# Memory gates kept in SBUF until the output stage, with other buffers, accumulators and preparation order there

## The chip, the cores and the metric

The kernel runs on one core of a Trainium2 chip. The metric is the device time of one execution in microseconds (us). Before the change three runs gave 604.79, 606.60 and 608.34 us. One further execution was profiled; its own time is 606.42 us, and the span of its trace is 604.6 us, so 1.8 us lie outside the span.

## The reference, cut to what matters

```
def merge(x, fox_o, gf, pool_o, gp, mem_o, gm, w_out):
    cat = concatenate([silu(gf) * fox_o,      # 512 columns, forgetting attention
                       silu(gp) * pool_o,     # 256 columns, pooling mixer
                       silu(gm) * mem_o])     # 256 columns, memory attention
    return x + cat @ w_out                    # then y = rmsnorm(., g_final)
```

There are 1024 prompt rows and 64 sample rows of width 1024. One input projection gives queries, keys, values, forget gates, the pooling path and the three gates gf, gp, gm. Eight forgetting-attention heads (prompt rows causal over 1024 keys, sample rows over 512 cached keys and their own), four memory heads and the pooling mixer give 1024 columns in all; these are gated, multiplied by w_out, added to x and normalised. All of it is float32.

## The kernel before, in words

Each float32 matrix product is made of products of rounded halves: every operand is split into a high part (names ending in `hi`, or `wh`, `xh`, `chi`) and a low part (`lo`, `wl`, `xl`, `clo`), and three matmuls per block of 128 (high times high, high times low, low times high) are added up in PSUM.

Nothing is scheduled by hand. Every instruction goes to a `Planner` that records its reads and writes, then `flush` (line 189) places all instructions in one order by a cost model: at each step it takes the instruction that can start first on its engine, and among those that can start together the one with the lower `rank`, then the longer remaining path. `add` (line 94) gives rank -1 to matmuls into the PSUM pools `ps`, `pt` and `po`, and to work of other engines that touches pools `pp` or `wp`; all else has rank 0. The order is then fixed: each engine, and the DMA queue of SyncE (SP), takes its instructions one after the other and waits where one of them must wait. Tiles come from rings: a tile with 2 buffers can be written again when the readers of the tile two allocations earlier are done.

After the input projections and the attention heads, two things end the program. `proj2` (line 612) projects the two 128-column tiles of the memory gate gm, for three chunks of rows in the order `LAST` = (2, 1, 0): rows 768 to 1087, 256 to 767, 0 to 255. `gate_tile` (line 676) makes the gate: a multiply (`gr`, DVE), a Tanh (`gt`, ACT), a combine (DVE), and a store to DRAM (`gated`).

The output stage follows. `load_wout` (line 1204) loads w_out in three column blocks (blocks 1, 0 and 2 in that order; 256, 512 and 256 columns) in 8 pieces, and splits each into `wh` (ACT cast) and `wl` (a subtraction on POOL in two parts, or on DVE). These take the SBUF of the x halves, so block 1 can be written when chunk 2 of the projection is done, block 0 after chunk 1, block 2 after chunk 0. Raw pieces go by turns to a tile `wr` (one buffer) and to a `ptile` `Q` (three buffers).

`out_prep(t)` (line 1151) prepares a row tile t of 128 rows (t = 8 is the 64 sample rows) in two halves of four 128-column blocks: DMA of the attention results (`catd`), of the reciprocal row sums (`rsd`) and of the gates (`gated`), a multiply by the row sums (DVE), a multiply by the gates (POOL), a cast to `chi` (ACT) and a subtraction to `clo` (DVE). `chi` and `clo` take the `whi` and `wlo` rings of pool `wp`, two buffers each, which the projection weights use before. `out_tile(t)` (line 1231) does the matmuls into PSUM, for the columns in three steps (columns 768 to 1023, 0 to 511, 512 to 767), adds x (tile `xt`), sums squares (ACT), takes the root, scales and stores. Both accumulators of a tile come from pool `pp` (two banks). The tiles are taken in the order 8, 0, 1, ..., 7, and the last one ends with three separate steps.

Of the kernel before, what the change touches and what calls it, by code (L numbers as in the profile page):

```python
# [42 lines left out]
class Planner:  # L43
# [5 lines left out]
    def __init__(self, nc, tc):  # L49
        self.nc, self.tc = nc, tc  # L50
        self.ops = []
        self.acc = {}
        self.slots = {}
        self.alloc = {}
        self.users = {}
        self.home = {}
        self.free = {e: 0.0 for e in self.ENG}
        self.lock = {"vector": 0.0, "gpsimd": 0.0}
        self.mode = self.table = None
        self.dma = [0.0] * 16  # L60
        for e in self.ENG:
            setattr(self, e, _Eng(self, e))
# [31 lines left out]
    def add(self, eng, fn, args, kw):  # L94
# [12 lines left out]
        urgent = into & {"ps", "pt", "po"} if eng == "tensor" else "pp" in homes or "wp" in into  # L107
        op.rank = -1 if urgent else 0
        preds = set()
# [162 lines left out]
def tile_hymba_step(  # L272
# [45 lines left out]
    def half(par):  # L318
# [4 lines left out]
    md = [dram.tile([4 * HD, 2 * MEM], F32, name=f"md{j}") for j in range(2)]  # L323
    gated = [
        [dram.tile([r, n], F32, name=f"gated{r}_{t0}") for t0, n in CH] for r in (768, 256)
    ]
    catd = [dram.tile([D, 256 if c < 4 else NSA], F32, name=f"catd{c}") for c in range(5)]
# [347 lines left out]

    def gate_tile(r0):
        def f(acc, ci, t0, n):
            t = row("gr")
            nc.vector.tensor_tensor(t[:, :n], acc[:, :n], rb[:, t0 : t0 + n], op=ALU.mult)
            th = row("gt")  # L680
            nc.scalar.activation(th[:, :n], t[:, :n], AF.Tanh, scale=0.5)
            nc.vector.scalar_tensor_tensor(
                t[:, :n], th[:, :n], 1.0, t[:, :n], op0=ALU.add, op1=ALU.mult
            )
            g, r = divmod(r0, 768)
            nc.sync.dma_start(gated[g][ci][r : r + P, :n], t[:, :n])

        return f
# [462 lines left out]
    def out_prep(t):  # L1151
# [4 lines left out]
        hk = lambda x, w: x[:, : w * m].rearrange("p (k t) -> p k t", k=w)  # L1156
        ch = kv(wp.tile([P, WC], F32R, tag="whi", name=nm("chi")))
        if t < 8:
            cl = kv(wp.tile([P, WC], F32R, tag="wlo", name=nm("clo")))
        else:  # L1160
            cl = ch[:, :, m:]
        w = 512 // m
        rt = ptile()[:, : 6 * m].rearrange("p (k t) -> p k t", k=6)
        for par in (0, 1):
# [6 lines left out]
        for a in range(0, KT, w):  # L1171
            ct, gt = hk(ptile(512), w), hk(ptile(512), w)
            nc.sync.dma_start(
                ct, catd[t // 2][a * P : (a + w) * P, oc : oc + m].rearrange("(k p) t -> p k t", p=P)
            )
            for g, e0, e1 in ((0, 0, 6), (1, 6, 8)):
                b0, b1 = max(a, e0), min(a + w, e1)
                if b0 < b1:
                    nc.sync.dma_start(
                        gt[:, b0 - a : b1 - a, :],  # L1180
                        gated[g][ci][(b0 - e0) * P : (b1 - e0) * P, o : o + m].rearrange(
                            "(k p) t -> p k t", p=P
                        ),
                    )
            ks = slice(a, a + w)
            for b0, b1, o0 in ((0, 4, 0), (6, 8, 2)):
                b0, b1 = max(a, b0), min(a + w, b1)
                if b0 < b1:
                    c_ = ct[:, b0 - a : b1 - a, :]
                    nc.vector.tensor_tensor(c_, c_, rt[:, b0 - o0 : b1 - o0, :], op=ALU.mult)  # L1190
            nc.gpsimd.tensor_tensor(ct, ct, gt, op=ALU.mult)
            nc.scalar.activation(ch[:, ks, :m], ct, AF.Copy, scale=0.5)
            nc.vector.scalar_tensor_tensor(
                cl[:, ks, :m], ct, 0.5, ch[:, ks, :m], op0=ALU.mult, op1=ALU.subtract
            )
# [8 lines left out]
    def load_wout():  # L1204
        gfb.append(ap_.tile([P, UW], F32, tag="u", name="gfb", bufs=1)[:, :D])
        nc.sync.dma_start(gfb[0], gfin.unsqueeze(0).to_broadcast([P, D]))
        for ci in LAST:
# [6 lines left out]
            for i, k0 in enumerate(range(0, KT, kk)):  # L1214
                raw = ptile() if i % 2 else wp.tile([P, D], F32, tag="wr", name=nm("wr"), bufs=1)
                raw = raw.rearrange("p (k c) -> p k c", k=kk)
# [14 lines left out]
    def out_tile(t):  # L1231
# [17 lines left out]
        for pi, pc, o, w, full in steps:  # L1249
            if pi not in accs:  # L1250
                accs[pi] = ppt() if pi < 2 else pst()
            acc = accs[pi]
# [30 lines left out]
        for nh in (0, 1):  # L1283
# [9 lines left out]
            else:  # L1293
                nc.scalar.activation(xg[:, cols], xg[:, cols], AF.Copy, scale=r)
                nc.scalar.dma_start(y_o[c, cols], xg[:, cols])

    def project(name):
        kind, j = name[:-1], int(name[-1])
# [5 lines left out]
        elif kind == "k":  # L1304
            proj(TK + j, k_tile(j))
        elif kind == "gf":
            proj(TGF + j, gate_tile(j * P))
        elif kind == "qm":
            proj(TQM + j, q_tile(4 + j))
        elif kind == "u":  # L1310
            proj(TU + j, u_tile(j))
        elif kind == "gp":
            proj(TGP + j, gate_tile(512 + j * P))
        else:
            proj2(TGM, gate_tile(768), TGM + 1, gate_tile(768 + P))

# [32 lines left out]
    for _ in side[0]:  # L1349
        pass  # L1350
    load_wout()
    for t in order:
# [110 lines left out]
```

## Time and profile before

| what | us |
|---|---|
| runs: lowest, median, highest | 604.79, 606.60, 608.34 |
| the profiled execution, its own time | 606.42 |
| its span | 604.6 |
| TensorE (PE) busy | 570.9 (94%) |
| VectorE (DVE) busy | 336.1 (56%) |
| ScalarE (ACT) busy | 291.7 (48%) |
| GpSimd (POOL) busy | 219.9 (36%) |

The busy time of PE comes from pipelined matmuls whose ends are modelled; what a matmul costs in a row of them is seen from the distance of their starts. A timeline row gives start, duration, engine, operation, tiles, shape, count, and in brackets the idle time before it and what ended that. SPq is SyncE issuing DMAs; such a row includes the time in which the queue waited between two issues that are merged into it. In the trace every instruction has line 251 (the planner's emission), so rows are told apart by their tiles.

### The profile page before, as it was taken

How to read it: one execution, taken by the hardware profiler on the slowest of the kernel's cores; microseconds unless marked ns; L12 is line 12 of the kernel's file. 1: busy time of each engine (PE TensorE's matmuls, PEld its weight loads, DVE VectorE, ACT ScalarE, POOL GpSimd, SP SyncE). 2: the span in 40 equal slices, each digit the busy share in tenths (PEclk: the TensorE clock that was granted, in tenths of full speed). 3: DMA queues.
4: the chain of work that ended last, by engine and by line, in shares of the span. 5: the costliest groups of instructions: out<-in, count | busy, mean ns of one | idle time of the engine just before them, and what ended most of it. 6: DMA issues, size and time to landing. Idle time of an engine off the chain costs nothing.

```text
span 604.6 us, 11202 instructions
## 1 busy us (share of the span) xinstructions
PE 570.9 (94%) x3815; PEld 522.4 (86%) x3815; DVE 336.1 (56%) x822; ACT 291.7 (48%) x675; POOL 219.9 (36%) x356
## 2 busy tenths in 40 slices
PE   7899999999999999999999999999999759898994
PEld 5899998989989999989999888989998648897894
DVE  5774521113778787647598636753365644535534
ACT  6653721211777877778488526741243333212212
POOL 2401373464746442123466533321114551311210
PEclk9899999999999999999999999999999978999998
DMA  8998745479996975596768668533245495684621
GB/s 311 328 329 289 233 126 205 139 275 283 330 342 214 342 233 144 159 340 212 248 180 293 219 203 267 186 89 117 80 141 173 137 233 138 200 232 153 207 105 70
DMA packets 99764, 128.59 MB, mean 213 GB/s; under 512 B 30931, under 2 KB 71675, under 8 KB 98171
## 3 DMA queue, kind: packets, MB, share of 16 engines
q1 hardware_dynamic: 99418, 127.61, 65.7%
q8 instruction: 30, 0.49, 0.3%
q10 hardware_dynamic: 288, 0.27, 0.1%
q14 instruction: 28, 0.22, 0.1%
HBM read 87.52 MB, written 40.33 MB: 211 GB/s over the span
## 4 chain that ended last, share of the span: by engine, by line
PE 77%; DMA 9%; DVE 6%; ACT 3%; issue 2%; POOL 2%; SPq 1%; DVEq 0%; POOLq 0%; ACTq 0%
PE pp L251 49%; PE s L251 12%; PE o L251 9%; PE pt L251 7%; DMA nat<-in_xn_dram 2%; DMA xr<-in_xT_dram 1%; DMA nc<-gpd 1%; DVE xt L251 1%; DMA xt<-in_xn_dram 1%; DVE gr L251 1%; DMA wr<-in_wv_dram 1%; DMA kd<-hl 1%; SPq L251 1%; DVE s L251 1%; DMA ks<-kd 1%
## 5 line engine op out<-in xcount | busy, mean ns | idle before, releaser
L251 PE MATMUL pp<-xh,whi 128*128 128x320 f32 (+2 forms) x480 | 149.3, 333 | 3.3 <-DVE kr L251 1.6
L251 PE MATMUL pp<-xh,wlo 128*128 128x512 f32 (+2 forms) x480 | 148.4, 332 | 0.0
L251 PE MATMUL pp<-xl,whi 128*128 128x320 f32 (+2 forms) x480 | 147.8, 329 | 0.0
L251 POOL TENSOR_TENSOR wlo<-wr,whi 128x512 fp32r<-128x512 f32 (+2 forms) x44 | 60.1, 1386 | 110.8 <-ACT whi L251 94.3
L251 PEld LDWEIGHTS pp<-xh,whi 128*128 128x128 f32 x480 | 88.3, 189 | 11.3 <-DVE gr L251 2.2
L251 PEld LDWEIGHTS pp<-xh,wlo 128*128 128x128 f32 x480 | 88.3, 188 | 6.0
L251 PEld LDWEIGHTS pp<-xl,whi 128*128 128x128 f32 x480 | 88.4, 189 | 5.0
L251 PE MATMUL pp<-wh,chi 128*128 128x256 f32 (+1 forms) x208 | 65.7, 332 | 14.1 <-DVE chi L251 7.9
L251 DVE TENSOR_TENSOR plo<-pt,phi 128x512 fp32r<-128x512 f32 (+1 forms) x96 | 60.8, 642 | 20.7 <-ACT phi L251 16.1
L251 ACT CAST phi<-pt 128x512 fp32r<-128x512 f32 (+1 forms) x96 | 51.7, 550 | 30.3 <-PE pt L251 16.6
L251 PE MATMUL pp<-wl,chi 128*128 128x256 f32 (+1 forms) x208 | 65.4, 328 | 0.0
L251 PE MATMUL pp<-wh,clo 128*128 128x256 f32 (+1 forms) x184 | 56.7, 324 | 0.0
L251 PEld LDWEIGHTS pp<-wh,chi 128*128 128x128 f32 x208 | 39.7, 194 | 19.3 <-DVE chi L251 8.1
L251 PE MATMUL o<-plo,vs 128*128 128x256 f32 x160 | 49.9, 324 | 0.0
L251 ACT CAST whi<-wr 128x1024 fp32r<-128x1024 f32 (+1 forms) x25 | 24.6, 983 | 51.8 <-PE pp L251 49.5
L251 PE MATMUL o<-phi,vs 128*128 128x256 f32 x160 | 47.5, 305 | 0.0
L251 PE MATMUL pt<-ident,Q 128*128 128x128 f32 x248 | 47.3, 272 | 0.0
L251 POOL TENSOR_TENSOR P<-P,P 128x512 f32<-128x512 f32 x17 | 22.2, 1319 | 66.4 <-DVE P L251 58.5
L251 ACT ACTIVATE Q<-Q,m 128x576 f32<-128x576 f32 (+4 forms) x40 | 38.0, 950 | 13.2 <-DVE m L251 13.1
L251 PEld LDWEIGHTS pp<-wl,chi 128*128 128x128 f32 x208 | 39.6, 193 | 3.5
L251 PE MATMUL s<-ks,qb 128*128 128x512 f32 (+3 forms) x128 | 37.9, 374 | 0.4 <-DVE m L251 0.3
L251 PEld LDWEIGHTS pp<-wh,clo 128*128 128x128 f32 x184 | 34.3, 190 | 3.3 <-DVE clo L251 0.7
(239 smaller groups left out, 1221.2 us busy)
## 6 DMA issues: line engine op xcount, KB each, us to landing
qd<-hl SPq DMA_DIRECT2D x24, 576.0 KB, 6.3
wr<-in_wt_dram SPq DMA_DIRECT2D x20, 512.0 KB, 3.7
qa<-qd SPq DMA_DIRECT2D x12, 640.0 KB, 6.3
ks<-kd SPq DMA_DIRECT2D x8, 800.0 KB, 7.4
qb<-qd SPq DMA_DIRECT2D x12, 512.0 KB, 4.8
P<-catd SPq DMA_DIRECT2D x17, 256.0 KB, 3.0
nat<-in_xn_dram SPq DMA_DIRECT2D x8, 512.0 KB, 7.8
kd<-hl SPq DMA_DIRECT2D x16, 256.0 KB, 5.2
```

Of the source, the lines that this page charges most:

```text
L251: getattr(getattr(self.nc, op.eng), op.fn)(*op.args, **op.kw)
```

## The change

`gate_tile` gets an argument: with a tile `kept` it writes the combined gate there instead of storing it to DRAM. The gm gates of all rows stay in one tile `gmg` (ring `hl` of pool `rp`). In `out_prep` the gate multiply on POOL becomes two or three: the first six column blocks still come from DRAM, the last two are multiplied out of `gmg`. Six stores and nine loads of gm gates go.

The row-sum tile `rt` no longer takes a `Q` buffer but by turns the rings `vraw` and `qa` (one buffer each) of the attention. Each third tile in the order (1, 4, 7) takes `chi` and `clo` from the ring `vs` instead of `whi` and `wlo`. The raw w_out pieces with odd number take ring `nc` (two buffers) instead of `Q` (three). The accumulators of tile t come from pools `pp`, `ps`, `pt`, `po` in turn.

`out_prep(8)` is recorded ahead of `load_wout`, and from there on `calm` takes away the rank -1 of all instructions recorded later, so that only start time and remaining path decide. (`boost` is never set to true.)

```diff
@@ Planner.add
-        op.rank = -1 if urgent else 0
+        op.rank = -1 if self.boost or urgent and not self.calm else 0
@@ gate_tile
-    def gate_tile(r0):
+    def gate_tile(r0, kept=None):
...
+            out = t[:, :n] if kept is None else kept[:, t0 : t0 + n]
             nc.vector.scalar_tensor_tensor(
-                t[:, :n], th[:, :n], 1.0, t[:, :n], op0=ALU.add, op1=ALU.mult
-            )
-            g, r = divmod(r0, 768)
-            nc.sync.dma_start(gated[g][ci][r : r + P, :n], t[:, :n])
+                out, th[:, :n], 1.0, t[:, :n], op0=ALU.add, op1=ALU.mult
+            )
+            if kept is None:
+                nc.sync.dma_start(gated[ci][r0 : r0 + P, :n], out)
@@ out_prep
-        ch = kv(wp.tile([P, WC], F32R, tag="whi", name=nm("chi")))
+        spare = order.index(t) % 3 == 2
+        if spare:
+            ch = ap_.tile([P, KT, P], F32R, tag="vs", name=nm("chi"))
+        else:
+            ch = kv(wp.tile([P, WC], F32R, tag="whi", name=nm("chi")))
...
-        rt = ptile()[:, : 6 * m].rearrange("p (k t) -> p k t", k=6)
+        if order.index(t) % 2:
+            rt = ap_.tile([P, 2, 512 + P], F32, tag="qa", name=nm("rt"), bufs=1)
+        else:
+            rt = ap_.tile([P, 13, HD], F32, tag="vraw", name=nm("rt"), bufs=1)
...
-            nc.gpsimd.tensor_tensor(ct, ct, gt, op=ALU.mult)
+            c_ = ct[:, : e1 - a, :]
+            nc.gpsimd.tensor_tensor(c_, c_, gt[:, : e1 - a, :], op=ALU.mult)
+            if a + w > 6:
+                for i in (0, 1):
+                    c_ = ct[:, 6 - a + i, :]
+                    nc.gpsimd.tensor_tensor(
+                        c_, c_, kept[0][:, i, t * P : t * P + m], op=ALU.mult
+                    )
@@ load_wout
-                raw = ptile() if i % 2 else wp.tile([P, D], F32, tag="wr", name=nm("wr"), bufs=1)
+                raw = (
+                    nbt(NPR) if i % 2 else wp.tile([P, D], F32, tag="wr", name=nm("wr"), bufs=1)
+                )
@@ out_tile
-                accs[pi] = ppt() if pi < 2 else pst()
+                ring = (ppt, pst, ptt, otile)[order.index(t) % 4]
+                accs[pi] = ring() if pi < 2 else (pst if ring is ppt else ppt)()
@@ project
-            proj2(TGM, gate_tile(768), TGM + 1, gate_tile(768 + P))
+            gm_t = rp.tile([P, 2, NQ], F32, tag="hl", name="gmg", bufs=HB)
+            kept.append(gm_t)
+            proj2(TGM, gate_tile(0, gm_t[:, 0]), TGM + 1, gate_tile(0, gm_t[:, 1]))
@@ end of the program
+    nc.calm = True
+    nc.boost = False
+    prep[8] = out_prep(8)
+    nc.boost = False
     load_wout()
```

Apart from the output stage, from single loads and multiplies for it that are taken ahead into the last head's attention and the gate projections, and from a few neighbours on PE there that change places, every engine has the order it had. Three places follow, in the order in which the instructions stand. Numbers are buffer numbers: `wh0`, `wh1`, `wh2` are the blocks of w_out.

ACT and POOL where the output stage starts. In the rows before, `chi_1427` is tile 8 and `chi_1441` tile 0:

```order
L251 CAST wh0_2848<-Q_1424_2853 128x1024
L251 CAST wh2_2854<-Q_1426_2857 128x1024
L251 ACTIVATE gt_1415_2839<-gr_1414_2838 128x256
L251 ACTIVATE gt_1418_2842<-gr_1417_2841 128x256
L251 CAST wh0_2848<-wr_1423_2852 128x1024
L251 ACTIVATE chi_1427_2858<-P_1429_2860 128x8x64
L251 ACTIVATE chi_1441_2872<-P_1444_2875 128x512
L251 COPY ysl_1435_2866<-pp_1434_2865 64x512
```

Now, with `chi_1419` for tile 8, `chi_1441` for tile 0 and `chi_1456` for tile 1:

```order
L252 CAST wh0_2850<-nc_1428_2855 128x1024
L252 ACTIVATE chi_1441_2870<-P_1444_2873 128x512
L252 ACTIVATE chi_1419_2841<-P_1421_2843 128x8x64
L252 ACTIVATE gt_1415_2837<-gr_1414_2836 128x256
L252 ACTIVATE gt_1418_2840<-gr_1417_2839 128x256
L252 CAST wh2_2856<-nc_1430_2859 128x1024
L252 CAST wh0_2850<-wr_1427_2854 128x1024
L252 COPY ysl_1435_2864<-pp_1434_2863 64x512
L252 ACTIVATE chi_1456_2885<-P_1459_2888 128x512
```

Both casts to `chi` stand ahead of two w_out casts instead of behind them, and that of tile 1 stands behind the copy out of tile 8's accumulator. POOL stood so at the same place, with `P_1429` for tile 8 and `P_1444`, `P_1446` for tile 0:

```order
L251 TENSOR_TENSOR wl0_2849<-wr_1421_2850,wh0_2848 128x512 x2
L251 TENSOR_TENSOR wl0_2849<-Q_1424_2853,wh0_2848 128x512 x2
L251 TENSOR_TENSOR wl2_2855<-Q_1426_2857,wh2_2854 128x512
L251 TENSOR_TENSOR P_1429_2860<-P_1429_2860,P_1430_2861 128x512
L251 TENSOR_TENSOR wl2_2855<-Q_1426_2857,wh2_2854 128x512
L251 TENSOR_TENSOR wl0_2849<-wr_1423_2852,wh0_2848 128x512 x2
L251 TENSOR_TENSOR P_1444_2875<-P_1444_2875,P_1445_2876 128x512
```

And now (`P_1459` is tile 1):

```order
L252 TENSOR_TENSOR P_1421_2843<-P_1421_2843,P_1422_2844 128x384
L252 TENSOR_TENSOR wl0_2851<-wr_1425_2852,wh0_2850 128x512 x2
L252 TENSOR_TENSOR wl0_2851<-nc_1428_2855,wh0_2850 128x512 x2
L252 TENSOR_TENSOR wl2_2857<-nc_1430_2859,wh2_2856 128x512 x2
L252 TENSOR_TENSOR wl0_2851<-wr_1427_2854,wh0_2850 128x512 x2
L252 TENSOR_TENSOR P_1459_2888<-P_1459_2888,P_1460_2889 128x512
```

As before, `wl2` (block 2) stands ahead of the third piece of `wl0`. The gate multiply of tile 8 that stood between them, and that of tile 0's first half behind them, have moved ahead of all `wl0`.

PE at the start of the output stage. Before, all 16 matmuls of tile 8 into `pp_1434` came first and tile 0 after them:

```order
L251 MATMUL pp_1416_2840<-xh0_127,wlo_1400_2824 128x256
L251 MATMUL pp_1434_2865<-wh0_2848,chi_1427_2858 128x512
L251 MATMUL pp_1434_2865<-wl0_2849,chi_1427_2858 128x512
L251 MATMUL pp_1434_2865<-wh0_2848,chi_1427_2858 128x512
L251 MATMUL pp_1434_2865<-wl0_2849,chi_1427_2858 128x512
```

Now tile 0 (`s_1451`) and tile 8 (`pp_1434`) are mixed:

```order
L252 MATMUL pp_1416_2838<-xh0_124,wlo_1400_2822 128x256
L252 MATMUL s_1451_2880<-wh0_2850,chi_1441_2870 128x512
L252 MATMUL s_1451_2880<-wl0_2851,chi_1441_2870 128x512
L252 MATMUL s_1451_2880<-wh0_2850,clo_1442_2871 128x512
L252 MATMUL s_1451_2880<-wh0_2850,chi_1441_2870 128x512
L252 MATMUL s_1451_2880<-wl0_2851,chi_1441_2870 128x512
L252 MATMUL pp_1434_2863<-wh0_2850,chi_1419_2841 128x512
L252 MATMUL pp_1434_2863<-wl0_2851,chi_1419_2841 128x512
```

The order goes on with six more of tile 8, six of tile 0, then one of each (the fifth column block of tile 8 and the end of tile 0's fourth), the last seven of tile 8, twelve of tile 1 (into pool `pt`), four of tile 0's second half, and then the first that read `wh2`. Farther on, up to four tiles are under way together, where before there were two.

DVE at the end of the program. Before, tile 6 (`xt_1538`) had been added and half scaled when the additions of the last tile (`xt_1553`) came:

```order
L251 SCALAR_TENSOR_TENSOR xt_1538_2969<-xt_1538_2969,fr_1544_2975,gfb_2843 128x512
L251 TENSOR_TENSOR xt_1553_2984<-pp_1556_2987,xt_1553_2984 128x512
L251 TENSOR_TENSOR xt_1553_2984<-pp_1558_2989,xt_1553_2984 128x256
L251 TENSOR_TENSOR Q_1555_2986<-xt_1553_2984,gfb_2843 128x512
L251 TENSOR_SCALAR ss_1554_2985<-ss_1554_2985 128x1
L251 TENSOR_TENSOR Q_1555_2986<-xt_1553_2984,gfb_2843 128x256
L251 SCALAR_TENSOR_TENSOR ss_1554_2985<-ss_1554_2985 128x1 x2
L251 RECIPROCAL fr_1562_2993<-rt_1563_2994 128x1
L251 SCALAR_TENSOR_TENSOR fr_1562_2993<-fr_1562_2993,ss_1554_2985,rt_1563_2994 128x1
L251 RECIPROCAL fr_1562_2993<-fr_1562_2993 128x1
L251 TENSOR_SCALAR Q_1555_2986<-Q_1555_2986,fr_1562_2993 128x512
```

Now the end reads:

```order
L252 SCALAR_TENSOR_TENSOR ss_1554_2983<-ss_1554_2983 128x1
L252 RECIPROCAL fr_1544_2973<-rt_1545_2974 128x1
L252 SCALAR_TENSOR_TENSOR fr_1544_2973<-fr_1544_2973,ss_1539_2968,rt_1545_2974 128x1
L252 TENSOR_TENSOR Q_1555_2984<-xt_1553_2982,gfb_2845 128x256
L252 RECIPROCAL fr_1562_2991<-rt_1563_2992 128x1
L252 SCALAR_TENSOR_TENSOR fr_1562_2991<-fr_1562_2991,ss_1554_2983,rt_1563_2992 128x1
L252 RECIPROCAL fr_1562_2991<-fr_1562_2991 128x1
L252 RECIPROCAL fr_1544_2973<-fr_1544_2973 128x1
L252 SCALAR_TENSOR_TENSOR xt_1538_2967<-xt_1538_2967,fr_1544_2973,gfb_2845 128x512 x2
L252 TENSOR_SCALAR Q_1555_2984<-Q_1555_2984,fr_1562_2991 128x512
```

Ahead of these rows stand five additions together, two of tile 6 (512 columns each) and three of tile 7 (512, 256, 256), and the root's small steps. The scaling of tile 6 in two halves now stands between the last small steps and the last instruction. On PE the last matmuls of tiles 6 and 7 are mixed up to the end, in all three column steps of tile 7.

More of the change, by code (lines that the diff above doesn't have):

```diff
@@ L59, in __init__ @@
         self.mode = self.table = None
+        self.calm = self.boost = False
         self.dma = [0.0] * 16
@@ L323, in tile_hymba_step @@
     md = [dram.tile([4 * HD, 2 * MEM], F32, name=f"md{j}") for j in range(2)]
-    gated = [
-        [dram.tile([r, n], F32, name=f"gated{r}_{t0}") for t0, n in CH] for r in (768, 256)
-    ]
+    gated = [dram.tile([768, n], F32, name=f"gated_{t0}") for t0, n in CH]
     catd = [dram.tile([D, 256 if c < 4 else NSA], F32, name=f"catd{c}") for c in range(5)]
@@ L1156, in out_prep @@
         hk = lambda x, w: x[:, : w * m].rearrange("p (k t) -> p k t", k=w)
-        ch = kv(wp.tile([P, WC], F32R, tag="whi", name=nm("chi")))
+        spare = order.index(t) % 3 == 2
[3 more added lines that the diff above has]
+            ch = kv(wp.tile([P, WC], F32R, tag="whi", name=nm("chi")))
         if t < 8:
-            cl = kv(wp.tile([P, WC], F32R, tag="wlo", name=nm("clo")))
+            if spare:
+                cl = ap_.tile([P, KT, P], F32R, tag="vs", name=nm("clo"))
+            else:
+                cl = kv(wp.tile([P, WC], F32R, tag="wlo", name=nm("clo")))
         else:
@@ L1162, in out_prep @@
         w = 512 // m
-        rt = ptile()[:, : 6 * m].rearrange("p (k t) -> p k t", k=6)
+        if order.index(t) % 2:
+            rt = ap_.tile([P, 2, 512 + P], F32, tag="qa", name=nm("rt"), bufs=1)
+            rt = rt.rearrange("p a b -> p (a b)")
+        else:
+            rt = ap_.tile([P, 13, HD], F32, tag="vraw", name=nm("rt"), bufs=1)
+            rt = rt.rearrange("p a b -> p (a b)")
+        rt = rt[:, : 6 * m].rearrange("p (k t) -> p k t", k=6)
         for par in (0, 1):
@@ L1175, in out_prep @@
             )
[L1176 to L1183, printed above, removed]
-                    )
+            e1 = min(a + w, 6)
+            nc.sync.dma_start(
+                gt[:, : e1 - a, :],
+                gated[ci][a * P : e1 * P, o : o + m].rearrange("(k p) t -> p k t", p=P),
+            )
             ks = slice(a, a + w)
@@ L1295, in out_tile @@
                 nc.scalar.dma_start(y_o[c, cols], xg[:, cols])
+    kept = []
     def project(name):
```

## The prediction

> **What bounds the kernel now.** I read the slices of the span first, to see where TensorE (PE) stops, then PE's timeline there, then the other engines' rows at the same time.
>
> ```profile
> span 604.6 us, 11202 instructions
> PE   7899999999999999999999999999999759898994
> PEclk9899999999999999999999999999999978999998
> ```
>
> A slice is 15.1 us. PE is at its limit in almost all of them. The change leaves the order alone up to the end of the gate projection, so what counts is the end: the dip in slices 32 and 33 (484 to 514 us), the small ones behind, and the last slice. PE's rows name them:
>
> ```profile
> 479.87 0.39 PE L251 MATMUL pp<-xh,wlo 128*128 128x256 f32 x2
> 488.16 0.80 PE L251 MATMUL pp<-wh,chi 128*128 128x512 f32 x1 [7.90 <-DVE chi L251]
> ...
> 498.36 0.57 PE L251 MATMUL pp<-wh,chi 128*128 128x512 f32 x1 [1.75 <-ACT chi L251]
> ...
> 507.72 0.47 PE L251 MATMUL pp<-wh,chi 128*128 128x512 f32 x1 [0.87 <-DVE xt L251]
> ...
> 526.96 0.36 PE L251 MATMUL pp<-wh,chi 128*128 128x256 f32 x1 [1.97 <-DVE xt L251]
> ...
> 544.96 0.51 PE L251 MATMUL pp<-wh,chi 128*128 128x512 f32 x1 [0.78 <-DVE xt L251]
> ...
> 557.22 0.51 PE L251 MATMUL pp<-wh,chi 128*128 128x512 f32 x1 [0.78 <-DVE xt L251]
> ...
> 596.65 0.28 PE L251 MATMUL pp<-wh,clo 128*128 128x256 f32 x1
> ```
>
> The gaps are 7.90 + 1.75 + 0.87 + 1.97 + 0.78 + 0.78 = 14.05 us. The first is the start of the output stage, waiting for a `chi`; the four behind `DVE xt` are full accumulator banks that DVE has not emptied. After the first two, PE also ran slowly:
>
> ```profile
> 491.74 0.44 PE L251 MATMUL pp<-wh,chi 128*128 128x512 f32 x1
> 502.28 0.28 PE L251 MATMUL pp<-wl,chi 128*128 128x256 f32 x1
> 500.00:502.00 2.00, 2.00 (x6) 1.54 (x6) 1.10 (x2) 0.00 (x0) 0.76 (x1) 0.50 0.64 171
> ```
>
> The last row is a window (PE, weight loads, DVE, ACT, POOL, clock, DMA share, GB/s): the granted clock is 0.50 with PE busy throughout. What a matmul costs at full clock is the distance of starts:
>
> ```profile
> 468.94 0.63 PE L251 MATMUL pp<-xh,wlo 128*128 128x512 f32 x2
> 469.40 0.63 PE L251 MATMUL pp<-xh,whi 128*128 128x512 f32 x2
> 478.92 0.40 PE L251 MATMUL pp<-xl,whi 128*128 128x256 f32 x2
> ```
>
> Two 512-wide ones take 0.46 to 0.47 us, 0.234 each; 256-wide, eight from 478.92 to 479.87 take 0.95, 0.118 each. From 488.16 to 491.74 eight 512-wide matmuls took 3.58 instead of 1.87 us: 1.7 lost. From 498.36 to 502.28 ten took 3.92 instead of 2.34: 1.6 lost. So the losses are 14.05 + 1.7 + 1.6 = 17.35 us.
>
> The stage's work: tile 8 has 16 of 512 and 32 of 256 columns, 7.5 us; each other tile 24 and 48, 11.28 us; with eight of them 97.8 us. The projection's last slot ends at 480.1, the last matmul at 596.77: 116.65 us = 97.8 work + 17.35 losses + 1.5 unnamed. Behind it comes a tail of 604.6 - 596.8 = 7.8 us.
>
> **The change part by part.**
>
> *The start.* These are the rows on which it hangs:
>
> ```profile
> 480.30 1.04 ACT L251 CAST wh<-Q 128x1024 fp32r<-128x1024 f32 x1 [2.50 <-PE pp L251]
> 485.17 1.05 ACT L251 CAST wh<-wr 128x1024 fp32r<-128x1024 f32 x1 [2.95 <-DMA wr<-in_wout_dram]
> 486.12 0.62 ACT L251 ACTIVATE chi<-P 128x512 fp32r<-128x512 f32 x1
> 480.63 0.74 DVE L251 TENSOR_TENSOR gr<-pp,rb 128x256 f32<-128x256 f32 x2
> 486.78 1.32 DVE L251 SCALAR_TENSOR_TENSOR chi<-P,chi 128x512 fp32r<-128x512 f32 x1 [1.66 <-ACT chi L251]
> 491.85 0.69 DVE L251 SCALAR_TENSOR_TENSOR clo<-P,chi 128x512 fp32r<-128x512 f32 x1 [2.06 <-ACT chi L251]
> 478.42 4.82 POOL L251 TENSOR_TENSOR wl<-Q,wh 128x512 fp32r<-128x512 f32 x3
> 486.29 2.95 POOL L251 TENSOR_TENSOR wl<-wr,wh 128x512 fp32r<-128x512 f32 x2
> 479.04 2.04 SPq L251 DMA_DIRECT2D gated<-gr  x2
> 481.13 0.43 SPq L251 DMA_DIRECT2D wr<-in_wout_dram  x1
> 481.13 4.02 DMA wr<-in_wout_dram
> ```
>
> Before, `chi` at 486.12 stands behind the cast at 485.17, which waits for a piece of w_out issued at 481.13 behind two gate stores. Now tile 0's `chi` stands directly behind the cast of 480.30 and needs the `whi` ring, free at 480.3: done at about 481.0. DVE is free at 481.4 and makes `clo`, which takes 0.69 alone and 1.32 while POOL writes; I take 1.0, 482.4. Tile 8 follows by 483.1. PE then has 21 matmuls that need only the first two pieces of block 0: 4.9 us, to about 487.
>
> The third piece of `wl0` comes next. POOL's first two subtractions of the 4.82 row end at 481.7 (1.6 each). Then come two for `wl2`, whose cast waits for both Tanhs, at about 483.4 to 486.6, and two for `wl0`, 486.6 to 489.6 (row 486.29). PE gets half at 488.1, the rest at 489.6, and finishes tile 8's first step at about 490.8.
>
> ```profile
> 493.84 0.58 ACT L251 COPY ysl<-pp 64x512 f32<-64x512 f32 x1 [2.02 <-PE pp L251]
> 494.45 0.68 DVE L251 TENSOR_TENSOR xt<-ysl,xt 64x512 f32<-64x512 f32 x1 [1.91 <-ACT ysl L251]
> 499.28 1.22 DVE L251 TENSOR_TENSOR wl<-wr,wh 128x1024 fp32r<-128x1024 f32 x1 [0.25 <-ACT wh L251]
> ```
>
> Tile 1's `chi` has been put behind the `ysl` copy, so PE waits 0.58 + 0.63 more: 1.2 to 1.5 us, to 492.2; its `clo` stands behind an `xt` addition of 0.68 and comes in time. One stretch at half clock is likely after these gaps; it cost 1.7 and 1.6 above, and I take 1.0 because the gaps are shorter. The last piece of block 2 goes into `wr` once POOL is done with it (489.6), lands at 493.4 by the 4.02 row, is cast by 495.9 and subtracted by 497.2, before PE needs it. By 498.5 PE has done 48 matmuls of 512 and 3 of 256 columns, 11.6 us. Lost since 480.1: 498.5 - 480.1 - 11.6 = 6.8 us. Before, the same two places lost 7.90 + 1.75 + 1.7 + 1.6 = 13.0 us. Bounds: about 3 (PE starts at 482.4 and loses 0.7 more) and 13.0 (nothing gained).
>
> By the Trainium skill, page "TensorE: Matmul & The Clock Gate", section "HAM oscillation — how this bites in real kernels", only idle gaps over about 3.4 us throttle the clock, and the sum would lose the 1.0, giving 597.8 us. The window above at 0.50, behind a gap of 1.75, speaks against it, and the row decides.
>
> *Accumulators.* Four pools in turn give eight banks where `pp` gave two. The four waits behind `DVE xt` (0.87 + 1.97 + 0.78 + 0.78 = 4.4 us) need DVE to lag by more than three tiles now, so they go. What can come instead is a half that is prepared late:
>
> ```profile
> P<-catd SPq DMA_DIRECT2D x15, 256.0 KB, 3.0
> xt<-in_xn_dram SPq DMA_DIRECT2D x7, 512.0 KB, 5.0
> L251 POOL TENSOR_TENSOR P<-P,P 128x512 f32<-128x512 f32 x16 | 20.9, 1315 | 66.2 <-DVE P L251 58.2 <-DMA out_dram<-xt 8.0
> ```
>
> A half takes 3.0 (load) + 0.7 (DVE) + 1.3 (POOL) + 0.63 (ACT) + 0.7 (DVE) = 6.3 us, and PE needs 11.3 for a tile's two halves, with later ones begun ahead. The tightest place I find is DVE's emptying of tile 1, which waits for an `xt` load of 5.0 us or more, with `clo` of tiles 4 and 5 queued behind on DVE: slack about 1 us. So the later waits lie between 0 and the 4.4 of before; I take 0.7, nearer to 0, since a half has 5 us to spare.
>
> *Gates in SBUF.* Six stores and nine loads go. On the path I price that at nothing: the load of the attention results, 3.0 us, stays and lands beside the gates. It is in the sum only through the start, where SP's 2.04 us at 479.04 goes. POOL's multiply per tile grows from 2 x 1.31 to one of that and one split in three, a little under 3 us of 11.3: hidden; unhidden it would be some 0.3 per tile, 2.4 in all. Tile 8's and 0's multiplies moved ahead of the stage cost DVE and POOL 0.7 and 1.3 us beside PE at work; they are taken as 0, with 2.0 if that cover is gone.
>
> *The row-sum tile, `vs` and `nc`.* Other rings, same instructions; they only let loads start earlier. Nothing.
>
> *The tail.*
>
> ```profile
> 592.54 0.75 DVE L251 SCALAR_TENSOR_TENSOR xt<-xt,fr,gfb 128x512 f32<-128x512 f32 x1
> 600.01 0.49 DVE L251 TENSOR_SCALAR Q<-Q,fr 128x512 f32<-128x512 f32 x1
> 600.53 0.33 SPq L251 DMA_DIRECT2D out_dram<-Q  x1
> ```
>
> Tile 6 is now finished together with tile 7. Between DVE's last small step and the last scaling (0.49) stand tile 6's two scalings, 2 x 0.75 = 1.5 us, and its own small steps, some 0.7; two stores of `xt` are issued by SP ahead of the last (0.33 each). The last issue to the end, 604.6 - 600.53 = 4.1 us, stays. Against that the last matmuls are spread over two tiles, so some additions come sooner. Bounds: 0 to 1.5 + 0.7 + 0.7 = 2.9; I take 2.3, for the scalings surely lie on the path. Tail: 10.1 us.
>
> *Sum.* 480.1 + 97.8 + 1.5 + 6.8 + 0.7 = 586.9 for the last matmul, + 10.1 = 597.0 against 604.6: -7.6 us. The profiled execution took 606.4, within 0.2 of the median of the runs (606.6), so the forecast is 606.4 - 7.6 = **598.8 us**. Its own range is 594 to 602.5: half of the way to the bounds of the start (-1.9, +3.1) and of the tail and the late halves, one way at a time.
>
> **The rivals.**
>
> *The start is not won.* If the w_out pieces and not `chi` end the wait, the new early matmuls only move the gap to the third `wl0` piece and to tile 1. For it: in the row of 486.29 that subtraction ends at 489.2, and I place it at 489.6, no earlier. Against it: 21 matmuls are free of that piece. At the old loss, 13.0 instead of 6.8, the time is 598.8 + 6.2 = 605.0 us.
>
> *More is won.* No slow clock (-1.0), no late half (-0.7), the piece of `wl0` 1.0 earlier, and a tail that grows by 0.6 instead of 2.3 (-1.7): 598.8 - 4.4 = 594.4 us. For it: eight banks let PE take other tiles' matmuls. Against: the order on PE is fixed, it cannot step past a waiting one.
>
> *Slower: a stall per tile.* Without rank -1 for `chi`, `clo` and the emptying of banks, these stand in DVE's queue behind whatever could start first in the planner's costs, such as an addition that waits for its `xt` load (6.69 us in the worst case of the row below). Each such stall costs what the one at 498.36 did, 1.75 and 1.6 at half clock, 3.35 us. With six of the eight tiles that is 598.8 + 20.1 = 619 us; the sign turns at 7.6/3.35, between two and three tiles. Against it: halves have 5 us to spare.
>
> ```profile
> 519.35 6.69 DMA xt<-in_xn_dram
> ```
>
> *The gates' saving does nothing.* Likely, and priced so: 598.8 stays.
>
> *The clock.* The Trainium skill, same page, section "A second HAM failure mode: psum-queue depth-cycling", says that cycling through PSUM banks makes the clock swing. Four pools in turn are such cycling. From the rows, a matmul at half clock costs (491.74 - 488.16)/8 = 0.45 instead of 0.234; half of the 97.8 us so is (0.45/0.234 - 1) x 48.9 = 45 more, 598.8 + 45 = 644 us. Against it: `proj2` already alternates between two accumulators at 468.94 to 469.40 at the full pitch.
>
> **How the numbers follow.** Forecast 0.58; start not won 0.20; more won 0.09; stall per tile 0.11; clock 0.02. Runs of this kernel spread so that 0.5%, 3.0 us, is about what can be told from no change: faster is below 603.6, slower above 609.6. Faster: 0.58 + 0.09 + a quarter of the start case, 0.05 = 0.72. Same: 0.13 of the start case. Slower: 0.11 + 0.02 + 0.02 of the start case = 0.15. For 8 in 10 the range takes the forecast's own, most of the two neighbours, 592 to 608, and leaves the stalls and the clock out.
>
> **What would show it.** Right: PE's first output matmul at 482 to 483 instead of 488.16, on `s` with `chi` of tile 0; a short wait at about 487 to 490 behind POOL `wl`; no wait of PE behind `DVE xt` after 505; the last matmul at 585 to 588; then DVE's two `xt` scalings ahead of the last `Q`, and 9 to 11 us to the end. Wrong: a gap of several us behind ACT or DVE `chi` in the middle tiles, a clock of 0.5 in windows behind 510, a first matmul later than 486, or the last matmul past 592.

## The result and the profile after

The changed kernel takes 598.59 us (median of 4 runs, 596.5 to 599.49) against 607.0 us for the kernel before on the same chip: a ratio of 0.9848, 95% interval 0.9818 to 0.9877. Run again later, beside new runs of the kernel before, it gave 595.97 against 607.68 us, 0.9816 (0.9791 to 0.9841). The forecast was 598.8 us. That the number fits says little yet: its terms have to be compared one by one.

The head of the page of the changed kernel, one slice being 14.9 us:

```profile
span 596.4 us, 11206 instructions
PE   7789999999999999999999998999999988999993
PEclk9999999999999999999999999999999998999998
```

PE's timeline around the start of the output stage, with the last matmul of the projection, all waits behind it, and the last matmul of the program:

```profile
482.11 0.40 PE L252 MATMUL pp<-xh,wlo 128*128 128x256 f32 x2
482.93 0.51 PE L252 MATMUL s<-wh,chi 128*128 128x512 f32 x1 [0.42 <-ACT chi L252]
...
484.69 0.50 PE L252 MATMUL s<-wh,clo 128*128 128x512 f32 x1 [1.02 <-DVE clo L252]
...
491.02 0.50 PE L252 MATMUL pp<-wl,chi 128*128 128x512 f32 x1 [0.94 <-POOL wl L252]
...
493.65 0.50 PE L252 MATMUL pt<-wh,chi 128*128 128x512 f32 x1 [1.20 <-ACT chi L252]
...
494.69 0.65 PE L252 MATMUL pt<-wh,clo 128*128 128x512 f32 x1 [0.31 <-DVE clo L252]
...
586.51 0.28 PE L252 MATMUL s<-wh,clo 128*128 128x256 f32 x1
```

The first wait is now 0.42 us instead of 7.90, and behind 495 there is none up to the last matmul: the four behind `DVE xt` are gone. From 494.69 the matmuls run at half clock until 498.3, as in the window of 496 to 498 (clock is the third number from the right):

```profile
496.00:498.00 2.00, 2.00 (x6) 1.62 (x5) 1.01 (x3) 1.56 (x2) 0.00 (x0) 0.50 1.15 268
```

At the end, VectorE and SyncE:

```profile
586.27 1.01 DVE L252 TENSOR_TENSOR xt<-pp,xt 128x512 f32<-128x512 f32 x2
...
590.37 1.41 DVE L252 SCALAR_TENSOR_TENSOR xt<-xt,fr,gfb 128x512 f32<-128x512 f32 x2
591.70 0.48 DVE L252 TENSOR_SCALAR Q<-Q,fr 128x512 f32<-128x512 f32 x1
591.15 1.01 SPq L252 DMA_DIRECT2D out_dram<-xt  x2
592.21 0.63 SPq L252 DMA_DIRECT2D out_dram<-Q  x1
```

Tile 6's two scalings stand between tile 7's last small steps and its last scaling, and its stores ahead of the last store.

For all kernels I split the span in the same three: the end of the projection's last slot; the loss of the output stage (from there to the end of the last matmul's slot, less 97.8 us of work); the tail from there to the span's end. These are from one profile each; the ratios are from repeated runs, each against the kernel before on its own chip.

| kernel | projection ends | loss | tail | ratio (95% interval) |
|---|---|---|---|---|
| before | 480.1 | 18.9 | 7.8 | 1 |
| changed | 482.35 | 6.5 | 9.8 | 0.9848 (0.9818 to 0.9877) |
| changed, run again | 481.7 | 5.0 | 9.7 | 0.9816 (0.9791 to 0.9841) |
| without the accumulator pools | 480.2 | 12.7 | 7.6 | 0.9874 (0.9842 to 0.9905) |
| without the buffers | 479.7 | 11.1 | 9.7 | 0.9857 (0.9829 to 0.9885) |
| without calm | 479.5 | 10.5 | 11.7 | 0.9874 (0.9846 to 0.9902) |
| gates through DRAM | 481.4 | 10.2 | 10.3 | 0.9865 (0.9832 to 0.9898) |
| accumulator pools alone | 480.6 | 14.5 | 8.4 | 0.9918 (0.9895 to 0.9942) |
| early tile 8 and calm alone | 482.3 | 15.6 | 7.9 | 0.9961 (0.9942 to 0.9981) |
| buffers alone | 479.4 | 14.1 | 7.8 | 0.9930 (0.9906 to 0.9954) |
| third piece of block 0 in `Q` | 479.75 | 1.8 | 9.7 | 0.9748 (0.9728 to 0.9767) |
| last tile's matmuls last | 480.25 | 6.2 | 8.25 | 0.9776 (0.9754 to 0.9797) |
| both of these | 482.35 | 1.5 | 7.45 | 0.9720 (0.9698 to 0.9742) |
| both, and row sums reckoned later | 481.7 | 2.95 | 7.6 | 0.9750 (0.9732 to 0.9768) |

The kernels of rows 4 to 7 ran on one chip, those of rows 3 and 8 to 10 on a second, the next three on a third, the last on a fourth. The ratios of rows 4 to 7 lie close to both measurements of the changed kernel: all four intervals overlap that of the first, and against the second only those without the accumulator pools and without calm lie clear of it, by 0.0001 and 0.0005. So the times alone do not settle what undoing a part costs (0.5 to 3.5 us); the waits in the timelines say more.

### The profile page after: what moved, and what is told of

Its sections match the earlier page's. It is cut to its first block, busy times and chain, and to the rows that moved or that the text cites. A ratio compares the mean times of both kernels' runs of the same rounds, so it can differ in the third digit from the quotient of the medians.

```text
span 596.4 us, 11206 instructions
## 1 busy us (share of the span) xinstructions
PE 567.7 (95%) x3815; PEld 519.5 (87%) x3815; DVE 334.9 (56%) x822; ACT 291.5 (49%) x675; POOL 225.8 (38%) x374
## 4 chain that ended last, share of the span: by engine, by line
PE 77%; DMA 8%; POOL 4%; DVE 4%; issue 3%; ACT 2%; SPq 1%; DVEq 0%; ACTq 0%; POOLq 0%
PE pp L252 38%; PE s L252 15%; PE o L252 13%; PE pt L252 12%; DMA nat<-in_xn_dram 4%; POOL wl L252 2%; DMA rt<-rsd 1%; POOL wlo L252 1%; DMA kd<-hl 1%; DMA xr<-in_xT_dram 1%; DMA ks<-kd 1%; SPq L252 1%; DVE s L252 1%; POOL s L252 1%; DVE xt L252 0%
## 5 line engine op out<-in xcount | busy, mean ns | idle before, releaser
L252 PEld LDWEIGHTS pp<-xh,whi 128*128 128x128 f32 x480 | 88.3, 188 | 11.2 <-DVE gr L252 2.2
L252 ACT CAST phi<-pt 128x512 fp32r<-128x512 f32 (+1 forms) x96 | 51.8, 550 | 31.7 <-PE pt L252 18.9
L252 POOL TENSOR_TENSOR P<-P,P 128x512 f32<-128x512 f32 (+2 forms) x17 | 18.9, 1114 | 49.0 <-DMA P<-catd 27.8
L252 PEld LDWEIGHTS pt<-ident,Q 128*128 128x128 f32 x248 | 32.2, 140 | 3.1
L252 PEld LDWEIGHTS o<-plo,vs 128*128 128x128 f32 x160 | 30.3, 189 | 2.2 <-DVE plo L252 1.3
L252 PEld LDWEIGHTS o<-phi,vs 128*128 128x128 f32 x160 | 30.3, 189 | 1.4
L252 DVE CUSTOM_DVE_ANT_0 Q<-s,nc 128x512 f32<-128x512 f32 (+2 forms) x40 | 24.0, 601 | 11.4 <-PE s L252 8.1
L252 DVE TENSOR_TENSOR gr<-pp,rb 128x512 f32<-128x512 f32 (+2 forms) x24 | 12.6, 533 | 31.4 <-PE pp L252 31.3
L252 PE MATMUL pt<-ident,P 128*128 128x128 f32 x152 | 28.9, 272 | 0.0
```

The source lines that it names most:

```text
L252: getattr(getattr(self.nc, op.eng), op.fn)(*op.args, **op.kw)
```

## Experiments: one part undone

My theory was the prediction's sum: start, bank waits, tail. The rivals are in the expectations.

**Accumulators back in `pp`.**

```diff
-                ring = (ppt, pst, ptt, otile)[order.index(t) % 4]
-                accs[pi] = ring() if pi < 2 else (pst if ring is ppt else ppt)()
+                accs[pi] = ppt() if pi < 2 else pst()
```

> The changed kernel with its accumulators back in two banks of pool pp (its other parts kept). The four bank waits of the kernel before (0.87 + 1.97 + 0.78 + 0.78 = 4.4 us) come back: 598.6 + 4.4 = 603.0 us if the rings do only that. My theory adds that the rings also let PE fill the start with tile 0 while the third wl0 piece is missing (ready at about 491): with 16 matmuls of tile 8 first, PE has 12 of them and then waits, 2 to 3 us more, so 605 to 606 us. Rival, that the rings do nothing because the waits move to another engine: 598.6 us.

Measured 600.89 us, 0.9874. PE's timeline:

```profile
487.42 0.80 PE L252 MATMUL pp<-wl,chi 128*128 128x512 f32 x1 [1.46 <-POOL wl L252]
...
503.21 0.51 PE L252 MATMUL pp<-wh,chi 128*128 128x512 f32 x1 [0.78 <-DVE xt L252]
...
539.02 0.36 PE L252 MATMUL pp<-wh,chi 128*128 128x256 f32 x1 [1.70 <-DVE xt L252]
...
551.25 0.51 PE L252 MATMUL pp<-wh,chi 128*128 128x512 f32 x1 [0.78 <-DVE xt L252]
```

Three bank waits are back, and the start waits longer behind `wl`: the loss grows by 6.2 us against the first profile of the changed kernel. But the tail is 2.2 us shorter: with two banks PE takes tile 6 to its end before tile 7. The clock was 0.50 from 483.5 to 493.7, which is part of the grown loss. The time lies between the rival's 598.6 and the theory's 603 or 605 to 606 us: I had not counted that the accumulator pools also make the longer tail, and in this profile the projection ended 2.2 us earlier than in the first of the changed kernel.

**Buffers back.**

```diff
-        if order.index(t) % 2:
-            rt = ap_.tile([P, 2, 512 + P], F32, tag="qa", name=nm("rt"), bufs=1)
...
+        rt = ptile()[:, : 6 * m].rearrange("p (k t) -> p k t", k=6)
-        spare = order.index(t) % 3 == 2
+        spare = False
-                    nbt(NPR) if i % 2 else wp.tile([P, D], F32, tag="wr", name=nm("wr"), bufs=1)
+                raw = ptile() if i % 2 else wp.tile([P, D], F32, tag="wr", name=nm("wr"), bufs=1)
```

> The changed kernel with the row-sum tile and the odd raw pieces back in ring Q and with chi and clo always in the two buffers of whi and wlo (rings of accumulators, gates in SBUF, early preparation and calm kept). Theory: the early start comes from these buffers, since with Q shared the multiply of tile 0 cannot be taken ahead; tile 0's chi then stands behind two w_out casts again, PE starts with 9 matmuls of tile 8 and waits several us for them, 602 to 605 us, and the wait on DVE for the row sums ahead of 455 is smaller. Rival, that the order of preparation (tile 8 recorded first, calm) brings the start: 598 to 600 us.

Measured 600.32 us, 0.9857: less than the theory's 602 to 605, at the rival's upper end. There is a long wait behind `chi`, but it is not quite the one that the theory spoke of:

```profile
493.35 0.50 PE L252 MATMUL s<-wh,chi 128*128 128x512 f32 x1 [3.40 <-ACT chi L252]
495.14 0.58 PE L252 MATMUL pp<-wh,chi 128*128 128x256 f32 x1 [1.06 <-ACT wh L252]
```

PE starts with nine matmuls of tile 8 at 481.99 and waits only 0.9 us (by the distance of starts) for the first half of tile 0 at 485.08. The 3.40 us are for tile 0's second half: on POOL its gate multiplies stand behind four subtractions for `wl` (484.33 to 489.98) and end at 492.63. The loss is 4.6 us above that of the changed kernel. In the spans 2.7 us of this is hidden, since the projection ended that much earlier here than in the first profile of the changed kernel; more on that below.

**Without calm** (tile 8 still recorded first).

```diff
-    nc.calm = True
     nc.boost = False
     prep[8] = out_prep(8)
```

> The changed kernel without calm: rank -1 stays for accumulator matmuls and for work on pp and wp, tile 8 is still recorded ahead of load_wout. On PE and DVE the end is then in order again, tile 6 scaled before tile 7 is added, so the tail goes from 9.8 back to about 7.8 us; the start is the same up to small things. Theory: 598.6 - 1.9 = 596.7 us, with the same wait of DVE for the row sums ahead of 455. Rival, that calm keeps chi and clo of the middle tiles in time: gaps of 1 to 3 us behind chi or clo come up in the middle, 599 to 602 us.

Measured 601.09 us, 0.9874. PE's timeline bears out the rival for the middle (waits of 1.26 us behind `chi` at 518.83 and 1.06 behind `clo` at 565.90), and the shorter tail that I expected turned into a longer one:

```profile
587.40 0.41 SPq L252 DMA_DIRECT2D xt<-in_xn_dram  x1
591.55 1.02 DVE L252 TENSOR_TENSOR xt<-pp,xt 128x512 f32<-128x512 f32 x2 [4.61 <-issue]
```

The last tile's `xt` is loaded only at 587.40, behind stores that free its buffer, and the additions wait for it until 591.55. So calm, which costs the tail the interleaving, protects it from this.

**Gates through DRAM.** `gate_tile` stores all of its tiles again, `out_prep` loads eight blocks of gates, and one POOL multiply does each half:

```diff
-            if kept is None:
-                nc.sync.dma_start(gated[ci][r0 : r0 + P, :n], out)
+            g, r = divmod(r0, 768)
+            nc.sync.dma_start(gated[g][ci][r : r + P, :n], t[:, :n])
...
-            proj2(TGM, gate_tile(0, gm_t[:, 0]), TGM + 1, gate_tile(0, gm_t[:, 1]))
+            proj2(TGM, gate_tile(768), TGM + 1, gate_tile(768 + P))
```

> The changed kernel with the gm gates stored to DRAM and loaded again as before, all else kept. Theory (the prediction's zero): the transfers lie beside PE's work, 598.6 us within 1.0. Rival, that the stores ahead of the w_out load on SP matter: the third wl0 piece comes 2.0 us later and the time is about 600.6 us.

Measured 600.87 us, 0.9865. SyncE, POOL and PE of this kernel:

```profile
478.05 2.04 SPq L252 DMA_DIRECT2D gated<-gr  x2
481.99 0.38 SPq L252 DMA_DIRECT2D nc<-in_wout_dram  x1
482.47 0.45 SPq L252 DMA_DIRECT2D wr<-in_wout_dram  x1
...
489.22 3.12 POOL L252 TENSOR_TENSOR wl<-wr,wh 128x512 fp32r<-128x512 f32 x2
...
490.72 0.50 PE L252 MATMUL pp<-wl,chi 128*128 128x512 f32 x1 [1.85 <-POOL wl L252]
```

And of the changed kernel:

```profile
480.72 0.37 SPq L252 DMA_DIRECT2D wr<-in_wout_dram  x1
...
487.82 3.15 POOL L252 TENSOR_TENSOR wl<-wr,wh 128x512 fp32r<-128x512 f32 x2
```

Counted from each one's end of the projection, the load of `wr` is issued at +1.1 instead of -1.6 us, and the third piece of `wl0` ends at +11.0 instead of +8.6. The time came out near the rival's, and its mechanism is there: the stores ahead of the load delay the piece for which PE waits, now twice (a second wait of 0.94 us stands at 492.39). By the distance of starts the two are 2.0 + 1.1 us instead of 1.1. The loss grew by 3.7 us, though; most of the rest goes with the clock, which was 0.50 for 10.2 us here (491.6 to 501.9) instead of 3.4. Further on no wait of PE is named for a gate's load.

## Experiments: one part alone

**Accumulator pools alone**, in the kernel before.

> The kernel before with only the accumulators in four pools. Both chi still stand behind the cast that waits for a piece of w_out, so the start stays at 488 with its loss of 13.3 us. Theory: the four bank waits go, 1.0 + 2.1 + 1.0 + 0.8 = 5.0 us by the distance of starts, and the time is 602 us. Rival, from the four runs above, in which undoing any one part cost only 0.5 to 1.6 us: the parts stand in for each other, and the rings alone give all that they can, 4 to 6 us, or the wait moves to chi and they give under 2 us, 605 us.

Measured 602.95 us, 0.9918: 5.0 us of 607, the theory's value. All four bank waits are gone; the start is as before (`489.67`, a wait of 8.91 us behind `DVE chi`).

**Early tile 8 and calm alone.**

> The kernel before with only the early recording of tile 8 and calm. On ACT, tile 8's chi now stands ahead of the third cast of block 0, tile 0's still behind it, and on POOL a half of wl0 has fallen behind tile 0's multiply. Theory: PE starts at about 484 but waits for wl0 until about 493, so the start gains 1 to 3 us and the four bank waits stay: 604 to 606 us. Rival, that the order of preparation is the whole of the start's gain: 600 us.

Measured 605.19 us, 0.9961: 2.4 us, the theory's time, but not all of its terms.

```profile
485.81 0.80 PE L252 MATMUL pp<-wh,chi 128*128 128x512 f32 x1 [3.39 <-DVE chi L252]
...
490.89 0.80 PE L252 MATMUL pp<-wl,chi 128*128 128x512 f32 x1 [0.55 <-POOL wl L252]
...
498.05 0.58 PE L252 MATMUL pp<-wh,chi 128*128 128x256 f32 x1 [1.63 <-ACT wh L252]
```

PE starts earlier, but then stands behind `wl` and `wh` in turn, and the clock was 0.50 from 484.9 to 502.0. Of the four bank waits, which the theory kept, only two are left (0.78 us each, at 543.76 and 556.04).

**Buffers alone.**

> The kernel before with only the buffers changed (row sums, spare chi and clo, raw pieces). On ACT both chi stand ahead of the cast that waits, as in the changed kernel, so PE starts at 481 to 483; tile 8's 16 matmuls come first and wait for the third wl0 piece once or twice (1.5 + 0.5 us in the run without rings). Theory: the start loses about 7 to 8 instead of 13.3 us, the bank waits (5.0) stay: 601 us. Rival, that tile 8 must be recorded early for it: 606 us.

Measured 603.79 us, 0.9930: 4.2 us, below the theory's 6. PE starts at 481.75, then waits 1.59 us at 487.40 behind `POOL wl`, 1.83 at 496.18 behind `ACT chi`, and in two stretches up to 491.9 the matmuls stand 0.43 us apart. The four bank waits stay, at 3.2 us by the distance of starts. So the rival falls: for an early start tile 8 need not be recorded early, the buffers alone bring it. They are not needed for it either: in the kernel without the buffers, where tile 8 is recorded early, PE started at 481.99.

The three alone give 5.0 + 2.4 + 4.2 = 11.6 us; all together, with the gates, 9.2 and 11.2 in the two measurements. So no part needs the others to gain something. Whether they add up in full is open: each of the three has an interval of 1.2 to 1.5 us to either side, and the gates alone were not run.

## Experiments: the changed kernel again, and mended

**The changed kernel once more**, unedited.

> The changed kernel itself once more, on the chip of the runs below. In its first profile the projection ended 2.2 us later than in the kernel before, 1.5 of it because DVE stood behind a load of row sums that took 8.27 us. Theory: that load is only sometimes so slow (two kernels with the same order on DVE there showed a wait of 0.7 and 0.9 and no delay of PE), so the projection ends at 480 to 480.8 now, and what lies behind it, losses of 6.5 and a tail of 9.8 us, stays: a span of 594 to 595 us. Rival: the wait belongs to the change: the end at 482 again and a span of 596.4.

Measured 595.97 us and a span of 594.2. The span came as the theory had it, but not for its reason: the theory had the projection end at 480 to 480.8 and the loss stay at 6.5 us. The late row sums stand in the first profile's chain of waits as

```profile
443.83 8.27 DMA rt<-rsd
```

and in its timeline of DVE and PE as

```profile
452.18 0.69 DVE L252 TENSOR_TENSOR P<-P,rt 128x512 f32<-128x512 f32 x1 [2.40 <-DMA rt<-rsd]
453.53 0.39 PE L252 MATMUL o<-plo,vs 128*128 128x256 f32 x1 [0.94 <-DVE plo L252]
```

They did not hold up PE this time. Yet the projection ended at 481.7, for waits spread over the whole program. What shrank is the loss, by 1.5 us to 5.0, since the clock stayed up in the same window:

```profile
496.00:498.00 2.00, 2.00 (x11) 1.67 (x11) 1.43 (x2) 1.05 (x1) 0.00 (x0) 1.00 0.91 230
```

**The third piece of block 0 in its own buffer.** The single `wr` is free for it only when POOL has done the first piece.

```diff
-                raw = (
+                raw = ptile() if c == 0 and i == 2 else (
                     nbt(NPR) if i % 2 else wp.tile([P, D], F32, tag="wr", name=nm("wr"), bufs=1)
                 )
```

> The changed kernel with the third raw piece of w_out block 0 in a buffer of Q instead of the single buffer wr, so that its load no longer waits for POOL's first subtraction. Base: the changed kernel at 596.0 us on this chip, before at 607.7. Theory: that piece of wl0 is what ends PE's wait of 1.1 us behind POOL and holds up the copy of tile 8 and with it tile 1's chi (1.4 + 0.5 us); on POOL it now comes second, so these 3.0 us shrink to 0.5 to 1.5 and the time is 593.5 to 594.5 us. Rival: POOL itself is the limit there (eight subtractions of 1.3 to 1.8 us without a pause), the wait only moves to another of its pieces: 596 us.

Measured 592.15 us, 0.9748, better than either expected. Of PE's waits in the whole stage only two are left:

```profile
480.33 0.50 PE L252 MATMUL s<-wh,chi 128*128 128x512 f32 x1 [0.42 <-ACT chi L252]
...
482.09 0.50 PE L252 MATMUL s<-wh,clo 128*128 128x512 f32 x1 [1.02 <-DVE clo L252]
```

Tile 1's wait for `chi` and `clo` went along, so that piece stood behind two terms of my sum, not one. The slow clock behind it did not come up either; that alone shows little, since it was also absent from the second profile of the unedited kernel.

**The last tile's matmuls last**, through a higher rank for them on PE:

```diff
+        if self.after and eng == "tensor":
+            op.rank = 1
...
     for t in order:
+        nc.after = t == order[-1]
         out_tile(t)
```

> The changed kernel with the matmuls of the last tile behind all others that can start at the same time. Tile 6 is then added before tile 7's last matmuls end and of its scaling only one half stands ahead of the last instruction on DVE. Theory: the tail of 9.7 us loses tile 6's additions, small steps and one scaling, 1.5 us, 594.5 us. Rival: as without calm, the last tile's load of x comes late on SP and the tail stays or grows: 596 to 598 us.

Measured 594.52 us, 0.9776; the tail is 8.25 us, 1.5 less, as the theory had it.

**Both.**

> Both edits at once. Theory: they lie at opposite ends of the stage and add up: 596.0 - 2.0 - 1.5 = 592.5 us. Rival: no more than the better of the two, 594 us.

Measured 590.59 us, 0.9720 (0.9698 to 0.9742), the best kernel here: 17 us below the kernel before. Loss 1.5 and tail 7.45 us. The time is below the theory's 592.5 because the first edit had given 3.8 and not 2.0 us; from the two measured gains, 3.8 + 1.5 us, one would expect 590.7, so the two edits add up.

**Both, and row sums reckoned 5 us later by the planner:**

```diff
+            op.extra = 5.0 if str(reads[0].tensor.name).startswith("rsd") else 0.0
...
-                op.lat = max(self.dma[: op.ways]) - op.end + 4.0
+                op.lat = max(self.dma[: op.ways]) - op.end + 4.0 + op.extra
```

> The kernel with both edits (590.6 us on this chip), and 5 us more that the planner reckons for a load of row sums to land. On DVE tile 0's first row-sum multiply then stands behind the last three plo of the attention instead of ahead of them; the start of the output stage keeps its order. Theory: PE's wait behind plo at 453.6, which two of four profiles with the changed kernel's order on DVE and PE there showed (0.94 and 1.29 us), belongs to that multiply and does not come up; since it is lost only in some executions, 0.5 to 1.0 us on the median: 589.6 to 590.1 us. Rival: the wait is replaced by a later chi of tile 0 at the start of the stage, 591 us or more.

Measured 592.21 us, 0.9750 (0.9732 to 0.9768): no gain; the interval overlaps that of the kernel with both edits. The wait behind `plo` did not come up, but the later row sums moved work in the stage too:

```profile
529.16 1.29 DVE L255 TENSOR_TENSOR xt<-o,xt 128x512 f32<-128x512 f32 x2 [4.49 <-PE o L255]
530.37 0.68 DVE L255 SCALAR_TENSOR_TENSOR clo<-P,chi 128x512 fp32r<-128x512 f32 x1
...
531.11 0.39 PE L255 MATMUL pp<-wh,clo 128*128 128x256 f32 x1 [1.15 <-DVE ss L255]
```

DVE, in fixed order, stands 4.49 us before an addition that needs PE's result, and a `clo` behind it comes 1.15 us late for PE. What the wait at 453.5 costs on the median stays open: the edit did not take it away alone.

## Why the prediction was right, and where its terms were not

- **The start** held. Counted from the projection's end, tile 0's `chi` was forecast for +0.9 and its `clo` for +2.3 us (481.0 and 482.4, from 480.1); PE had them at +0.6 (482.93 - 482.35) and +2.3 (484.69). The third `wl0` piece was forecast for +9.5 and came at +8.6; PE waited for it 1.1 us by the distance of starts. Tile 1's `chi` cost 1.35 us, forecast 1.2 to 1.5; its `clo`, which I had in time, cost another 0.48. Slow clock: 1.0 forecast, 1.65 in one profile and 0 in the other. In all 6.3 and 4.7 us lost instead of 6.8.
- **The bank waits** went, and the 0.7 us for late halves did not come up. The 1.5 us that I carried over as "unnamed" were mis-sized: 0.2 and 0.3 us are left. About 1.0 of them belonged to the waits. A bracket of 7.90 is a distance of 8.05 between the slots, one of 1.97 is 2.13, and the four bank waits were 5.0 us, not 4.4; the pools alone gave just these 5.0.
- **The tail** grew by 1.9 us (9.8 and 9.7 against 7.8); forecast 2.3. Ranking the last tile last gave 1.5 back.
- **Ahead of the stage** I had put zero, with 2.0 us if the cover was gone. In the first profile the projection ended 2.2 us later than before. About 1.2 of this, not the 1.5 of my expectation above, arose around the early row-sum multiply of tile 0: the matmul that stood at 450.43 is 1.0 us later now (451.41), the one at 454.87 is 2.2 later (457.08). I had priced this multiply by its 0.69 us on DVE and not by the load that it waits for. That this is part of the change is not shown as a cost on the median: kernels with the same order there ended the projection anywhere between 479.5 and 482.35, and the one edit against it did not pay.
- **The gates** I counted only through SyncE's 2.04 us at the start. The load issues 2.7 us earlier and 0.0017 to 0.0049 of the time (1 to 3 us) hang on it, the intervals overlapping; the rest of the saved transfers shows nothing.

So 7.6 us of forecast gain met 8.2 in the profiles, and the agreement is partly luck: behind the projection the gain was 10.4 us (losses -12.4, tail +1.9), 2.2 of it missing ahead of it.

Rival "the start is not won" is out: the start lost 6.3 and 4.7 us, not 13.0. "A stall per tile" did come up where calm was taken away, with 1.3 and 1.1 us, not 3.35, and the clock stayed at 1.00 behind both. By the Trainium skill, page "TensorE: Matmul & The Clock Gate", section "HAM oscillation — how this bites in real kernels", the rule is to leave PE no idle gap above about 3.4 us. Here the clock was 0.50 behind gaps of 1.35 and 0.48 us, and 1.00 behind the same two in the second profile of the same kernel. So to stay below 3.4 us is not enough here, and the measurement decides. The Trainium skill, same page, section "A second HAM failure mode: psum-queue depth-cycling", tells of a kernel that cycled through banks, in which PE idled shortly between groups of matmuls and the clock swung. That does not show here: with eight banks in turn, in both profiles of the changed kernel, PE had no wait from 500 on up to its last matmul, and the clock was 1.00 in every window from 500 to 588.

## What to carry to other kernels

Before a stage begins, ask for every engine in fixed order what stands ahead of the first instructions that the bottleneck needs, down to the buffer that delays a load: one raw buffer less to share took 0.9816 to 0.9748 (0.7%), as much as the buffers of this change gave alone. Compare two profiles by their stages and repeat one of them unchanged: kernels with nearly the same instructions there ended their first 480 us up to 2.9 us apart. Take waits from the distance of starts, not from the bracket alone.

## What the runs showed of the hardware

Whether a short wait halves the clock is not settled by its length: the changed kernel had 1.35 and 0.48 us of waiting at 492.3 to 494.7 and lost 1.65 us at clock 0.50 in one execution; with 1.36 and 0.45 us it lost nothing in another. The traces show more of it. In all fourteen profiles every stretch at 0.50, except the last, which the end of the span cuts, lasted 3.41, 6.83, 10.24 or 17.07 us, whole multiples of 3.41: the clock changes on a grid of 3.41 us, and where the grid lies differs between executions. Windows laid along it, two of the first profile of the changed kernel and two of the second (behind the length stands PE's busy time):

```profile
491.48:494.89 3.41, 1.89 (x8) 0.94 (x7) 1.79 (x3) 1.11 (x2) 3.41 (x4) 1.00 0.78 223
494.89:498.31 3.42, 3.42 (x9) 2.65 (x9) 1.67 (x4) 2.29 (x4) 0.07 (x1) 0.50 1.07 235
...
490.15:493.57 3.42, 1.97 (x7) 1.16 (x7) 1.55 (x3) 1.11 (x2) 3.42 (x5) 1.00 0.56 170
493.57:496.98 3.41, 3.12 (x14) 2.36 (x13) 1.89 (x4) 2.12 (x4) 0.77 (x1) 1.00 1.09 250
```

In the first, both waits fall into one window, PE is busy for 1.89 us of it, and the next window runs at 0.50; in the second the same waits are divided between two windows, the first has 1.97 us, and the clock stays. Of all such windows at 1.00 in the fourteen profiles, those with PE busy for less than 1.59 us were followed by 0.50 and those with more than 1.90 us by 1.00; between them it went either way. PE's busy time is modelled, so these two bounds are rough. A load of row sums (192 KB into 64 partitions) took 8.27 us in one execution, and DVE's wait for it ranged from 0.30 to 2.76 us among kernels with the same order there. Taking eight PSUM banks in turn did not slow PE: its clock was 1.00 from 500 to 588.
